# The last expert's first piece: two half loads cut by partitions, the second laid out in eight blocks of eight rows

## The chip, the core and the metric

The kernel runs on one core of one Trainium2 chip. The metric is device time in microseconds; three runs of the kernel before gave 1342.24, 1344.37 and 1346.36, a median of 1344.37. TensorE is PE in the rows, VectorE DVE, ScalarE ACT, GpSimd POOL, and SP is the engine whose queue issues the loads.

## The reference

One layer of a streaming encoder trunk on 256 tokens and 16 meta tokens of width 1024: a mixer (gated DeltaNet beside gated linear attention) and then a mixture of 64 experts, of which every token takes two. Of the mixture:

```python
def expert_block(args):
    xblk, e = args
    hid = jax.nn.silu(xblk @ w1[e]) * (xblk @ w3[e])
    return hid @ w2[e]
...
y = jnp.zeros((T, d), yb.dtype).at[stok].add(yb[slot] * sw[:, None].astype(yb.dtype))
...
return rmsnorm(h, norm_final)[:, N_META:]
```

Each expert has w1 and w3 of 1024 x 512 and w2 of 512 x 1024, all float32: 6 MB an expert, 403 MB for all 64.

## The kernel before

The mixer takes the first 400 us or so. Then comes a loop over the 64 experts (`for e in range(NE)`), which runs all of them, whatever the router chose, each on a small block of gathered tokens. The weights come through the tensor `wx`, which `layout` builds on the host as 64 experts x 3 pieces x 128 partitions x 4096 columns. Piece 0 holds the first half of the depth of w1 (columns 0 to 2047) and of w3 (2048 to 4095), piece 1 the second half of both, piece 2 holds w2. A piece is 2 MB: 16 KB on each of 128 partitions.

The pieces go in turn into a ring of ten buffers of 128 x 4096 (lateA to lateE, ring0 to ring4; the rows of the profile leave the number of a ring buffer out). `ring_load` issues one load or half of one from SP, `ring_more` issues as many as have a free buffer, and `ring_take` hands a piece over and gives its buffer back. Up to the last expert but one a piece is one DMA of 2 MB. The last expert's three pieces go in two halves of 1 MB each (`hf` is 0 or 1), cut by columns: for pieces 0 and 1 the halves are w1's and w3's 2048 columns, for piece 2 they are 512 output columns in each of its four blocks. Every DMA signals on one of eight semaphores in turn, and SP waits before an issue until the DMA eight places earlier has landed, and until the buffer has been read. So eight loads are in flight at most.

PE's work on the last expert, in the order in which it stands in the program: `up` on the first half of the depth (32 matmuls `h<-ring`, which read piece 0, both halves of it), 50 matmuls on zeros (`keep_warm`, `misc<-zero`), `up` on the second half of the depth (32 matmuls, which read piece 1), the gate (ACT, then DVE), one transposition, and then w2 in two halves (`y<-lateE` and `misc<-lateE` for the first 512 output columns, then `y<-lateE` and `h<-lateE` for the others), each followed by the sum into `acc`. After that come the final norm, which needs `norm_final` (loaded to `h`, issued last of the loads), and four stores.

The branch of `ring_load` that piece 0 of the last expert takes is the last one:

```python
        else:
            hs = slice(2048 * hf, 2048 * (hf + count))
            to, src = t[:, hs], src[:, hs]
```

Of the kernel before, what the change touches and what calls it, by code (L numbers as in the profile page):

```python
# [26 lines left out]
NE = 64  # L27
# [69 lines left out]
def _body(tc, a, dbg, stop, ctx, nc, V, S, G, PE):  # L97
# [62 lines left out]
    wx = a["wx"]  # L160
    nload, slab_dma, gathered, gather_after, lead, x_act, x_dve = [0], [None], [None], [None], [None], [None], [None]

    def after(cell):

        return tc.issue_after(cell[0].ins) if cell[0] is not None else ExitStack()
# [6 lines left out]
    def ring_load(n, count):  # L172

        e, part, hf = n // 6, n // 2 % 3, n % 2
        if e == SPARE // 6:
            part = (0, 2, 1)[part]
        if n == SPARE:
            ring[e, part] = [w2p.tile([P, 2048], F32, name="ys", bufs=1)]
        elif hf == 0 or n == SPARE + 1:
            slot = ring_free.pop(0)  # L180
            ring.setdefault((e, part), []).extend((slot[0].tile([P, 4096], F32, name=slot[1], bufs=1), slot))
        t = ring[e, part][-2 if n != SPARE else 0]
        src = wx[e, part]
        if n == SPARE:
            to, src = t, src[:, 0:2048]
        elif part == 2 and e == NE - 1:
            hs = slice(512 * hf, 512 * hf + 512)
            to, src = t.rearrange("p (j d) -> p j d", j=4)[:, :, hs], src.rearrange("p (j d) -> p j d", j=4)[:, :, hs]
        else:
            hs = slice(2048 * hf, 2048 * (hf + count))  # L190
            to, src = t[:, hs], src[:, hs]
        with after(slab_dma):
            nc.sync.dma_start(to, src)

    def ring_more(n=6 * NE, whole=True):
        while n and nload[0] < 6 * NE and (ring_free or (nload[0] % 2 == 1) != (nload[0] == SPARE + 1) or nload[0] == SPARE):
            i = nload[0]
            count = 2 if whole and i % 2 == 0 and i != SPARE and i < 6 * (NE - 1) else 1
            ring_load(i, count)
            nload[0] += count  # L200
            n -= 1
# [13 lines left out]
    def partC(n):  # L215
        used[0] += n
        assert used[0] <= 4096
        return lateC[:, used[0] - n:used[0]]
# [3 lines left out]
    small = acts.tile([P, 3 + 96 + 8 + 8], F32, name="small")  # L222
# [133 lines left out]
    rows = acts.tile([P, 16], F32, name="rows")  # L356
# [4 lines left out]
    src = [(h[:, 0], P, NM), (h[:, 1], P, NM + P), (xm, NM, 0)]  # L361
# [3 lines left out]
    for i in (2, 0, 1):  # L365
        x, n, col = src[i]
# [544 lines left out]
    half = acts.tile([P, 3], F32, name="half")  # L911
# [3 lines left out]
    for i in range(2):  # L915
        t = partC(256).rearrange("p (c x) -> p c x", c=2)
# [178 lines left out]
    for s in range(4):  # L1095
        p = [pip.tile([P, T], F32, name="ip") for _ in range(2)]
        for kh in range(2):
            wh, wl = parts(len(units) + 2 * s + kh, 4)
            slab_load(s0 + 2 * s + kh + SLABS - 2)
            src = slab_tile[s0 + 2 * s + kh]  # L1100
# [341 lines left out]
    for e in range(NE):  # L1442
        g, i = divmod(e, GR)
# [110 lines left out]
def blocks(w, k, n):  # L1554

    r, c = w.shape
    return w.reshape(r // (k * P), k, P, c // n, n).transpose(3, 0, 2, 1, 4).reshape(-1, P, k * n)


def layout(i):  # L1560

    small = np.concatenate([
        i["norm_head_dn"][0].reshape(1, P).T, i["norm_head_gla"][0].reshape(2, P).T,
        i["conv_dn"][0].reshape(4, 24, P).transpose(2, 1, 0).reshape(P, 96),
        i["norm_ffn"][0].reshape(KT, P).T,
        i["norm_mix"][0].reshape(KT, P).T], 1)
    rows = np.concatenate([np.broadcast_to(i[n], (P, i[n].shape[1])) for n in ("dt_bias", "a_log", "b_group", "b_router")], 1)
    w = i["w_in"][0]
    few = np.zeros((D, P), np.float32)
    few[:, 0:8], few[:, 32:40], few[:, 64:80] = w[:, O_A:O_A + 8], w[:, O_B:O_B + 8], w[:, O_LR:O_LR + 16]  # L1570
    w13 = [i[n][0].reshape(NE, 2, 4, P, 512).transpose(0, 3, 1, 2, 4).reshape(NE, P, 2, 2048) for n in ("w1", "w3")]
    wx = np.empty((NE, 3, P, 4096), np.float32)
    for part in range(2):
        for n in range(2):
            wx[:, part, :, 2048 * n:2048 * n + 2048] = w13[n][:, :, part]
    wx[:, 2] = i["w2"][0].reshape(NE, 4, P, D).transpose(0, 2, 1, 3).reshape(NE, P, 4096)
    out = {
        "x": i["x"], "meta_tokens": i["meta_tokens"], "norm_final": i["norm_final"], "small": small, "rows": rows,
        "w_in": blocks(np.concatenate([w[:, :O_A], w[:, I_GQ:O_LR], w[:, I_G1:]], 1), KT, P),
        "w_small": blocks(few, KT, P)[0],  # L1580
        "w_proj_dn": blocks(i["w_proj_dn"][0], KT, P), "w_proj_gla": blocks(i["w_proj_gla"][0], KT, P),
        "w_out": blocks(i["w_out"][0], 4, 256),
        "w_route": blocks(np.concatenate([i["w_group"][0], i["w_router"][0]], 1), KT, 72)[0],
        "w_alpha": np.concatenate([i["w_alpha"][0], i["b_alpha"]], 0), "wx": wx, "consts": CONSTS}
    return {k: np.ascontiguousarray(v) for k, v in out.items()}
# [17 lines left out]
```

## Time and profile before

| What | us |
|---|---|
| median of three runs (1342.24 to 1346.36) | 1344.37 |
| the profiled execution's own time | 1344.17 |
| its span in the trace | 1342.4 |
| PE busy | 1179.6 |
| DVE busy | 447.5 |
| ACT busy | 314.6 |
| POOL busy | 92.4 |

The time is the span and 1.8 us around it. PE is busy for 88% of the span, but its matmuls are pipelined and wait for weights in between; what set the end is read from the chain of waits, and for a change to the last loads from the last 80 us of it. A DMA's landing is the start of its issue on SP plus its time to landing.

### The profile page before, as it was taken

How to read it: one execution, taken by the hardware profiler on the slowest of the kernel's cores; microseconds unless marked ns; L12 is line 12 of the kernel's file. 1: busy time of each engine (PE TensorE's matmuls, PEld its weight loads, DVE VectorE, ACT ScalarE, POOL GpSimd, SP SyncE). 2: the span in 40 equal slices, each digit the busy share in tenths (PEclk: the TensorE clock that was granted, in tenths of full speed). 3: DMA queues.
4: the chain of work that ended last, by engine and by line, in shares of the span. 5: the costliest groups of instructions: out<-in, count | busy, mean ns of one | idle time of the engine just before them, and what ended most of it. 6: DMA issues, size and time to landing. Idle time of an engine off the chain costs nothing.

```text
span 1342.4 us, 24165 instructions
## 1 busy us (share of the span) xinstructions
PE 1179.6 (88%) x10513; PEld 760.3 (57%) x10513; DVE 447.5 (33%) x1007; ACT 314.6 (23%) x681; POOL 92.4 (7%) x163
## 2 busy tenths in 40 slices
PE   9999999999999998898878888788788878878776
PEld 8998999899997454344333434334343434334323
DVE  6689787656665222111110101111110111111101
ACT  5575565365441111101000000100000001010101
POOL 1016214502000000000000000000000000000000
PEclk8999999999999999999998898989998998999999
DMA  7633332333997999899999999999999999999995
GB/s 267 217 111 110 113 117 90 126 110 117 369 372 306 427 428 426 366 427 427 427 426 428 428 427 426 426 429 427 425 428 429 427 425 428 428 428 425 428 425 226
DMA packets 46287, 459.53 MB, mean 342 GB/s; under 512 B 5441, under 2 KB 5697, under 8 KB 20450
## 3 DMA queue, kind: packets, MB, share of 16 engines
q1 hardware_dynamic: 45890, 457.43, 83.4%
q8 instruction: 83, 1.36, 0.4%
q10 hardware_dynamic: 288, 0.52, 0.1%
q14 instruction: 26, 0.21, 0.0%
HBM read 456.89 MB, written 1.05 MB: 341 GB/s over the span
## 4 chain that ended last, share of the span: by engine, by line
DMA 44%; PE 15%; ACT 1%; DVE 1%; issue 0%; DVEq 0%; POOL 0%; SPq 0%
DMA ring<-wx 15%; DMA lateB<-wx 9%; DMA lateA<-wx 9%; DMA lateE<-wx 6%; PE acc L125 5%; PE h L125 4%; DMA lateC<-wx 3%; DMA lateD<-wx 3%; PE y L125 3%; PE misc L125 2%; ACT ys L116 1%; ACT sl L116 0%; DVE hid L1329 0%; PE misc L1334 0%; DVE hT L1336 0%
## 5 line engine op out<-in xcount | busy, mean ns | idle before, releaser
L125 PE MATMUL acc<-ys,wot 128*128 128x512 f32 x480 | 226.8, 615 | 27.6 <-ACT ys L116 26.9
L125 PEld LDWEIGHTS acc<-ys,wot 128*128 128x128 f32 x480 | 88.6, 195 | 155.6 <-issue 92.3
L1329 DVE SCALAR_TENSOR_TENSOR hid<-h,sc,sl 128x128 f32<-128x128 f32 x63 | 22.1, 350 | 451.6 <-ACT sl L116 451.6
L125 PE MATMUL ip<-xh,lateD 128*128 128x256 f32 (+2 forms) x784 | 162.3, 297 | 0.0
L116 ACT ACTIVATE sl<-h,sc 128x128 f32<-128x128 f32 x63 | 23.2, 368 | 481.5 <-PE h L125 476.1
L125 PE MATMUL h<-ring,xg 128*32 128x256 f32 x2048 | 124.9, 382 | 6.5 <-DMA ring<-wx 6.3
L125 PEld LDWEIGHTS ip<-xh,lateD 128*128 128x128 f32 x784 | 128.8, 194 | 1.9 <-issue 0.3
L125 PE MATMUL ip<-xl,lateD 128*128 128x256 f32 (+2 forms) x392 | 115.6, 295 | 0.0
L116 ACT ACTIVATE ys<-y,sc 128x512 f32<-128x512 f32 (+1 forms) x61 | 41.5, 680 | 280.4 <-PE y L125 280.4
L125 PEld LDWEIGHTS h<-ring,xg 128*32 128x32 f32 x2048 | 62.5, 110 | 74.7 <-issue 25.6
L108 DVE TENSOR_SCALAR ys<-y,sc 128x512 f32<-128x512 f32 x59 | 44.3, 750 | 167.7 <-PE y L125 167.7
L113 DVE TENSOR_TENSOR lateD<-slab,lateD 128x1024 fp32r<-128x1024 f32 x64 | 80.9, 1264 | 30.7 <-ACT lateD L116 29.4
L116 ACT ACTIVATE lateD<-slab 128x1024 fp32r<-128x1024 f32 x64 | 67.7, 1058 | 57.0 <-PE ip L125 54.7
L125 PE MATMUL y<-ring,hT 128*32 128x512 f32 x496 | 68.2, 667 | 14.4 <-DMA ring<-wx 14.0
L125 PEld LDWEIGHTS ip<-xl,lateD 128*128 128x128 f32 x392 | 75.8, 194 | 1.1 <-issue 0.3
L125 PEld LDWEIGHTS misc<-ohs,h 128*128 128x128 f32 x488 | 56.8, 191 | 22.2 <-issue 12.1
L125 PE MATMUL misc<-ohs,h 128*128 128x128 f32 x488 | 62.7, 281 | 6.4 <-DVE hT L1336 6.4
L156 POOL TENSOR_TENSOR rss<-rss,c 128x1 f32<-128x1 f32 x2 | 1.1, 556 | 925.2 <-DVE rss L103 925.2
L1334 PE MATMUL misc<-c,hid 128*128 128x128 f32 x64 | 20.8, 324 | 49.0 <-DVE hid L1329 49.0
L125 PE MATMUL ip<-xl,wh 128*128 128x256 f32 (+2 forms) x192 | 57.3, 298 | 0.0
L125 PE MATMUL ip<-xh,wh 128*128 128x256 f32 (+2 forms) x192 | 56.8, 296 | 0.0
L125 PE MATMUL ip<-xh,wl 128*128 128x256 f32 (+2 forms) x192 | 56.1, 292 | 0.0
(480 smaller groups left out, 1643.0 us busy)
## 6 DMA issues: line engine op xcount, KB each, us to landing
ring<-wx SPq DMA_DIRECT2D x90, 2048.0 KB, 39.2
lateA<-wx SPq DMA_DIRECT2D x19, 2048.0 KB, 39.2
lateD<-wx SPq DMA_DIRECT2D x19, 2048.0 KB, 39.2
slab<-w_in SPq DMA_DIRECT2D x72, 512.0 KB, 3.7
lateC<-wx SPq DMA_DIRECT2D x18, 2048.0 KB, 39.2
lateB<-wx SPq DMA_DIRECT2D x18, 2048.0 KB, 39.2
lateE<-wx SPq DMA_DIRECT2D x17, 2048.0 KB, 39.1
ring<-wx SPq DMA_DIRECT2D x12, 1024.0 KB, 8.9
```

Of the source, the lines that this page charges most:

```text
L108: e.tensor_scalar(out, in0, s1, None, op0=op0, **kw)
L113: return (eng or V).tensor_tensor(out, in0, in1, op)
L116: return S.activation(out, in_, func, **kw)
L125: return PE.matmul(out, lhsT, rhs, start=start, stop=stop, **kw)
L156: G.tensor_tensor(out, x, C(name, n)[:, :w], ALU.pow)
L1329: late_dve[0] = V.scalar_tensor_tensor(hid, ph[:, P:256], sc[:, 0:1], sl, op0=ALU.mult, op1=ALU.mult)
L1334: PE.transpose(p[:, 0:P], hid, ident)
```

## The change

Only the two loads of piece 0 of the last expert (`e == NE - 1`, `part == 0`) change. Before, each moved 128 partitions of 2048 columns, 8 KB a partition, from `wx`. Now they are cut by partitions: the first moves partitions 0 to 63 with all their 4096 columns (64 rows of 16 KB) from `wx`, the second partitions 64 to 127 from a new input `w_half`. That one has the shape 8 x 9 x 4096, of which 8 x 8 rows are filled and read: the ninth row of each block keeps the eight blocks from being one run of 64 rows. Both loads still move 1 MB into the same buffer, and PE reads it as before. `w_half` is the first of the kernel's inputs; `wx` keeps its own copy of the rows.

```diff
         elif part == 2 and e == NE - 1:
             hs = slice(512 * hf, 512 * hf + 512)
             to, src = t.rearrange("p (j d) -> p j d", j=4)[:, :, hs], src.rearrange("p (j d) -> p j d", j=4)[:, :, hs]
+        elif part == 0 and e == NE - 1:
+            to, src = t[64 * hf:64 * hf + 64], (src[0:64], a["w_half"][:, 0:8])[hf]
         else:
...
+    half = np.zeros((8, 9, 4096), np.float32)
+    half[:, 0:8] = wx[NE - 1, 0, 64:].reshape(8, 8, 4096)
     out = {
-        "x": i["x"], "meta_tokens": i["meta_tokens"], "norm_final": i["norm_final"], "small": small, "rows": rows,
+        "w_half": half, "x": i["x"], "meta_tokens": i["meta_tokens"], "norm_final": i["norm_final"], "small": small, "rows": rows,
```

On SP the end of the program, from the last piece of expert 62 on, stood like this before (a row ends with the shape that is written):

```order
L193 DMA lateD<-wx 128x4096
L193 DMA ring_10397<-wx 128x2048 x2
L193 DMA ring_10457<-wx 128x2048 x2
L193 DMA lateE<-wx 128x4x512 x2
L1482 DMA h<-norm_final 128x1024
```

And in the changed program, on the same engine from the same place:

```order
L195 DMA lateD<-wx 128x4096
L195 DMA ring_10397<-wx 64x4096
L195 DMA ring_10397<-w_half 64x1x4096
L195 DMA ring_10457<-wx 128x2048 x2
L195 DMA lateE<-wx 128x4x512 x2
L1484 DMA h<-norm_final 128x1024
```

Two rows have taken the place of one pair; nothing has moved past another instruction, here or on another engine.

## Rows read from the trace of the kernel before

**Rows 1.** The page: the chain of work that ended last, as shares of the span, by engine and by line.

```profile
DMA 44%; PE 15%; ACT 1%; DVE 1%; issue 0%; DVEq 0%; POOL 0%; SPq 0%
DMA ring<-wx 15%; DMA lateB<-wx 9%; DMA lateA<-wx 9%; DMA lateE<-wx 6%; PE acc L125 5%; PE h L125 4%; DMA lateC<-wx 3%; DMA lateD<-wx 3%; PE y L125 3%; PE misc L125 2%; ACT ys L116 1%; ACT sl L116 0%; DVE hid L1329 0%; PE misc L1334 0%; DVE hT L1336 0%
```

**Rows 2.** The same chain in order of time, its last 125 us: start and length in us, and what it was.

```profile
1219.21 39.30 DMA lateA<-wx
...
1258.59 40.24 DMA lateB<-wx
1298.84 0.14 issue
1298.97 2.02 PE y L125 x16
...
1301.78 7.13 PE acc L125 x16
1308.91 3.63 PE h L125 x64
...
1316.92 3.70 PE acc L125 x8
1320.62 1.86 PE h L125 x32
1322.48 2.90 PE misc L125 x50
1325.38 1.91 PE h L125 x32
...
1336.20 0.75 DVE xg L103
```

**Rows 3.** Stretches of 2 to 100 us: start and end, length, busy us of PE, PEld, DVE, ACT and POOL with their instructions, PE's granted clock, the mean busy share of the 16 DMA engines, GB/s.

```profile
900.00:1000.00 100.00, 79.74 (x702) 37.78 (x694) 15.50 (x33) 8.47 (x16) 0.00 (x0) 0.98 1.01 427
1100.00:1200.00 100.00, 84.48 (x701) 41.40 (x702) 16.06 (x35) 9.77 (x18) 0.00 (x0) 0.93 1.01 427
...
1318.00:1320.00 2.00, 2.00 (x6) 0.83 (x5) 0.00 (x0) 0.00 (x0) 0.00 (x0) 1.00 1.01 398
1320.00:1322.00 2.00, 2.00 (x30) 0.94 (x32) 0.00 (x0) 0.00 (x0) 0.00 (x0) 1.00 0.77 311
1322.00:1324.00 2.00, 2.00 (x41) 1.59 (x30) 0.00 (x0) 0.00 (x0) 0.00 (x0) 1.00 0.57 211
1324.00:1326.00 2.00, 2.00 (x40) 1.64 (x41) 0.00 (x0) 0.00 (x0) 0.00 (x0) 1.00 0.52 201
1326.00:1328.00 2.00, 1.25 (x24) 0.51 (x16) 0.28 (x1) 0.37 (x1) 0.00 (x0) 1.00 0.52 204
1328.00:1330.00 2.00, 1.40 (x17) 0.56 (x17) 0.38 (x3) 0.40 (x1) 0.00 (x0) 1.00 0.15 59
```

**Rows 4.** The timeline of SP, the last seven loads: start of the issue and its length in us. In this order: piece 0 of the last expert (two loads to a ring buffer), piece 1 (two), piece 2 (two to lateE), norm_final.

```profile
1278.13 0.33 SPq L193 DMA_DIRECT2D ring<-wx  x1
1284.19 0.33 SPq L193 DMA_DIRECT2D ring<-wx  x1
1289.12 0.33 SPq L193 DMA_DIRECT2D ring<-wx  x1
1293.96 0.33 SPq L193 DMA_DIRECT2D ring<-wx  x1
1298.90 0.66 SPq L193 DMA_DIRECT2D lateE<-wx  x1
1303.74 5.47 SPq L193 DMA_DIRECT2D lateE<-wx  x1
1309.32 1.84 SPq L1482 DMA_DIRECT2D h<-norm_final  x1
```

**Rows 5.** DMA issues in narrow stretches, one for each of those loads in the same order, and how many us it took from issue to landing; for the fourth of them (issued at 1293.96) the trace gives no landing.

```profile
ring<-wx SPq DMA_DIRECT2D x1, 1024.0 KB, 37.9
ring<-wx SPq DMA_DIRECT2D x1, 1024.0 KB, 34.3
ring<-wx SPq DMA_DIRECT2D x1, 1024.0 KB, 31.9
...
lateE<-wx SPq DMA_DIRECT2D x1, 1024.0 KB, 27.3
lateE<-wx SPq DMA_DIRECT2D x1, 1024.0 KB, 25.1
h<-norm_final SPq DMA_DIRECT2D x1, 512.0 KB, 20.7
```

**Rows 6.** The timeline of PE on the last expert: start and length in us, and in brackets the idle time before and who ended it.

```profile
1320.55 1.93 PE L125 MATMUL h<-ring,xg 128*32 128x256 f32 x32
1322.42 2.97 PE L125 MATMUL misc<-zero 128*128 128x128 bf16 x50
1325.31 1.93 PE L125 MATMUL h<-ring,xg 128*32 128x256 f32 x32
...
1328.83 0.64 PE L125 MATMUL y<-lateE,hT 128*32 128x256 f32 x8 [0.38 <-DVE hT L1336]
...
1331.63 0.64 PE L125 MATMUL y<-lateE,hT 128*32 128x256 f32 x8
```

**Rows 7.** The only load that writes a part of the partitions from many rows, 16 of 128: lateA from meta_tokens, issued at 0.71 us. Its row of the DMA issues (us to landing last), and the stretch in which it ran, with the columns of rows 3.

```profile
lateA<-meta_tokens SPq DMA_DIRECT2D x1, 64.0 KB, 2.1
...
1.70:2.20 0.50, 0.50 (x7) 0.50 (x6) 0.00 (x0) 0.49 (x2) 0.49 (x2) 1.00 0.47 131
```

## The prediction

> **What bounds the kernel now.** I read the chain of waits first. By engine, DMA has 44% of the span and PE 15%, and the lines of DMA are the loads of `wx` [rows 1]: over the experts the kernel waits for weights. The stretches say how: from 900 to 1000 us and from 1100 to 1200 us all 16 DMA engines are busy (share 1.01) and move 427 GB/s [rows 3]. There a megabyte costs 1,048,576 / 427,000 = 2.46 us, a 2 MB piece 4.91.
>
> But the change touches only the last expert's first piece, and what counts is whether the chain still goes through DMA there. It does not. In order of time the last DMA of the chain is the load of lateB, issued at 1258.59, 40.24 us long, over at 1298.84; from 1298.97 on the chain is PE, ACT and DVE to the end [rows 2]. [...] What follows is 43.6 us of compute to the end of the span at 1342.4, and it moves only if a load that was early becomes late.
>
> How early are they? Issue plus time to landing [rows 4, 5]: piece 0 lands at 1278.13 + 37.9 = 1316.0 and 1284.19 + 34.3 = 1318.5; piece 1 at 1289.12 + 31.9 = 1321.0 for its first half; piece 2 at 1298.90 + 27.3 = 1326.2 and 1303.74 + 25.1 = 1328.8; norm_final at 1309.32 + 20.7 = 1330.0. The second half of piece 1 has no landing in the trace; I put it halfway between its neighbours, at 1323.6. PE uses piece 0 from 1320.55, piece 1 from 1325.31, piece 2 from 1328.83 and 1331.63 [rows 6], and DVE norm_final at 1336.20 [rows 2]. The slacks are therefore 2.05 us, 1.7, 2.6, 2.8 and 6.2. PE shows no wait for a DMA at any of these places; ahead of piece 1 it runs its 50 matmuls on zeros from 1322.42 [rows 6].
>
> One more view matters: how the DMA engines finish. Their share is 1.01 up to 1320, falls to 0.77 and 0.57 up to 1324, stays at 0.52 for the two stretches to 1328 and is 0.15 in the last [rows 3]. A share of a half for 4 us says that about eight of the 16 engines were done with all loads by 1324 or earlier and the other eight still had to work to 1329: a leading and a lagging half, some 7 us apart. A load has landed when the slowest engine has done its part, so the landings above are those of the lagging half. The rows don't name the engines of either half.
>
> **The change, part by part.**
>
> *The first load*, 64 rows of 16 KB for 128 of 8 KB: the same megabyte. On 16 engines it is four rows of 16 KB each, the row length of the 2 MB pieces that stream at 427 GB/s [rows 3]. Cost 0.
>
> *The second load* on eight engines: 128 KB on each of these, nothing on the others. At 2.46 us for 64 KB an engine this is +2.46 us of work for the eight that get it and -2.46 us for the other eight, and all loads behind it in the queue (piece 1, piece 2, norm_final) shift with it on each engine. Two ends follow. If the eight are the leading half, they have 7 us to spare and the lagging half is relieved: landings from this load on come up to 2.46 us earlier. PE was not waiting, so the end gains 0. If the eight are, or contain some of, the lagging half, the landings come 2.46 us later: piece 0 at 1318.5 + 2.46 = 1320.96 against the use at 1320.55, +0.41; piece 1 at 1323.6 + 2.46 = 1326.06 against 1325.31, +0.75 in total and not on top of the first; piece 2 at 1328.66 and 1331.26 against 1328.83 + 0.75 and 1331.63 + 0.75, nothing more; norm_final at 1332.5 against 1336.2, nothing. So this term lies between 0 and +0.8 us. I take 0: the slack covers nearly all of either case. What hides the later landing is PE's own work, above all the 2.9 us of matmuls on zeros ahead of piece 1; without that cover the loaded lagging half would cost the whole 2.46.
>
> [...]
>
> *Issue on SP.* Two issues replace two. A plain load holds SP for 0.33 us, the loads of another form 0.66 and 5.47 [rows 4]; I take 0.33 to 0.66, with 5.47 as the bound. Even that ends at 1284.19 + 5.47 = 1289.66, and the next issue stood at 1289.12: it would slip by 0.5 us, with its data first wanted some 30 us later [rows 5]. Nothing behind it on SP but loads with that same lead. Below nothing the term cannot go: SP is on no part of the chain [rows 1]. Cost 0.
>
> *Order and waits.* No instruction changes place on any engine and no wait is added. The buffer is the same, and PE still waits for both loads. A store later waits for the semaphore that the second load signals, at 1338, long after. Cost 0.
>
> *A new input ahead of the others* moves where `wx` lies in memory. The two 100 us stretches read different parts of `wx` at the same 427 GB/s [rows 3], so I see no dependence on the place; bounds of 0.5% either way of the 870 us of expert stream, 4 us, go into the rivals.
>
> Sum against the profiled execution: 1344.17 + 0 (0 to 0.8). That execution lies 0.20 below the median, so against the median 1344.4, at most 1345.2.
>
> **The rivals.**
>
> 1. *Slower: the two cut loads share the way into the buffer.* Each writes only half of the partitions, and on the first all 16 engines write into 64 of them. If two engines that write to the same group of partitions take turns, a packet takes twice its time. For the lagging half the first load then takes 4.92 instead of 2.46 us (+2.46), and if the eight engines of the second load lag too, their 128 KB take up to 9.8 us instead of 2.46 (+7.4), since the others write their own loads to the same partitions meanwhile. Together +9.8: piece 0 would land at 1328.3, 7.8 us after its use at 1320.55, and the end would come 7.8 us later, at 1352.2. The rival decides from the point where the landing slips by more than the slack of 2.05 us, and beats 0.3% (4 us) from a slip of 6. Against it: the load of 16 rows to 16 partitions landed in 2.1 us and moved 131 GB/s over its half microsecond [rows 7], where an eighth of the partitions, taking turns, would give 427 / 8 = 53. For it: that load is tiny, 64 KB, and the megabytes behind one another here are not. It also needs the lagging engines among the eight; if the eight lead, the waiting falls on engines with 7 us to spare and the relieved ones are late by little more than their slack.
>
> [...]
>
> 2. *Faster: PE waits for these loads in most executions, only not in this one.* Then relieving the lagging half brings up to 2.46 us: 1344.4 - 2.5 = 1341.9. Against it stand slacks of 1.7 us and more at all places [rows 4 to 6]. It would stay within 0.3%.
>
> 3. *It doesn't do what it says:* the second load still runs on 16 engines. Then it is 64 KB an engine as before, and the time 1344.4.
>
> 4. *The place of `wx` in memory* changes the stream's rate by 0.5%: 1340 or 1348.
>
> **How the numbers follow.** Forecast (landings move, the end by 0 to 0.8 us): 0.72. Rival 1: 0.13. Rival 2: 0.07. Rival 3: 0.03. Rival 4: 0.05, half on each side. About 0.3% is what a measurement of this kernel can tell from no change; that is 4 us. Within it lie the forecast and rivals 2 and 3: 0.82. Slower by more: rival 1 and half of rival 4, 0.155, written 0.15. Faster by more: half of rival 4, 0.025, written 0.03. The predicted time is the forecast's 1344.4. The range takes in rival 2 at 1341.9, the forecast's 1345.2 and the scatter of the three runs around their median (about 2 us up): 1341.7 to 1347.4. Outside it are rival 1 and rival 4, 0.18.
>
> **What the profile after would show.** The chain's last DMA should again be the load of expert 61's last piece, over at about 1299, and PE's matmuls of the last expert should show no wait for a DMA, or one of under 1 us ahead of the first 32. The end of the loads tells the halves: if the leading half got the megabyte, the time in which the DMA share is near a half shrinks by some 5 us (one side +2.46, the other -2.46) and norm_final lands near 1327.6; if the lagging half got it, that stretch grows and norm_final lands near 1332.5. Rival 1 shows as a wait of several us for the ring buffer ahead of PE's first 32 matmuls and as GB/s well under 400 while other loads are still queued. Rival 2 would show the last expert's waits gone in a time that fell by 2 us. Rival 4 would show in the GB/s of 900 to 1200 us. I would be wrong if PE waits over 4 us for piece 0, or if the stream up to 1299 is not what it was.

## The result and the profile after

| What | before | after |
|---|---|---|
| median of six runs, us | 1341.57 (1338.76 to 1346.36) | 1357.79 (1352.58 to 1364.45) |
| ratio, with its 95% interval | | 1.0131 (1.0099 to 1.0163) |
| the profiled execution's own time, us | 1344.17 | 1359.62 |
| its span, us | 1342.4 | 1357.7 |

The change costs 16.2 us by the medians and 15.45 us between the two profiled executions. That is slower by four times what a measurement can tell from no change, and outside the predicted range. The ratio is estimated apart from the medians, here and in the experiments, and need not be their quotient. The first rival came true, at twice its price.

**Where the rate went.** Stretches of the kernel after, with the columns of [rows 3]:

```profile
900.00:1000.00 100.00, 80.31 (x724) 39.30 (x722) 15.31 (x34) 7.78 (x15) 0.00 (x0) 0.98 1.01 427
1100.00:1200.00 100.00, 85.22 (x702) 41.02 (x700) 15.41 (x33) 9.41 (x17) 0.00 (x0) 0.93 1.01 428
...
1296.00:1300.00 4.00, 3.14 (x14) 1.25 (x7) 0.75 (x1) 0.69 (x1) 0.00 (x0) 1.00 1.08 418
1300.00:1304.00 4.00, 4.00 (x11) 1.71 (x9) 0.00 (x0) 0.00 (x0) 0.00 (x0) 1.00 1.01 217
1304.00:1308.00 4.00, 2.37 (x34) 0.94 (x32) 0.00 (x0) 0.00 (x0) 0.00 (x0) 1.00 0.98 211
1308.00:1312.00 4.00, 2.37 (x32) 0.97 (x32) 0.24 (x1) 0.37 (x1) 0.00 (x0) 0.79 1.00 207
1312.00:1316.00 4.00, 0.48 (x1) 0.18 (x1) 0.41 (x2) 0.00 (x0) 0.00 (x0) 0.50 1.10 216
1316.00:1320.00 4.00, 0.00 (x0) 0.00 (x0) 0.00 (x0) 0.00 (x0) 0.00 (x0) 0.50 0.93 148
1320.00:1324.00 4.00, 3.66 (x16) 0.75 (x16) 0.00 (x0) 0.00 (x0) 0.00 (x0) 0.51 0.97 208
...
1332.00:1336.00 4.00, 1.56 (x16) 0.90 (x20) 0.00 (x0) 0.00 (x0) 0.00 (x0) 0.50 0.81 247
1336.00:1340.00 4.00, 4.00 (x59) 2.83 (x52) 0.00 (x0) 0.00 (x0) 0.00 (x0) 0.80 0.56 214
```

The expert stream is what it was: 427 and 428 GB/s. At 1300 us it breaks in two: the share of the DMA engines stays near 1.0, but they deliver 217 GB/s, 0.51 of 427. Engines that are busy all the time and move half as much have packets that take twice their time. The packets in the trace, which no view lists one by one, say so themselves: of the 86 packets of 16 KB that start from 1301 to 1308 us none took less than 1.02 us and the middle one 1.24, where the middle one of the kernel before, from 1280 to 1304 us, took 0.61. This is the reverse of what [rows 3] show at the end of the kernel before, where the GB/s fall with the share because half of the engines have nothing left to do. Reading the two last columns together tells the two apart.

**Which loads it took.** SP's timeline of the kernel after (start of the issue, its length), which answers to [rows 4]; lateB stands first to place this execution beside the other:

```profile
1254.24 0.33 SPq L195 DMA_DIRECT2D lateB<-wx  x1
...
1264.11 0.33 SPq L195 DMA_DIRECT2D lateA<-wx  x1
1268.91 0.33 SPq L195 DMA_DIRECT2D lateD<-wx  x1
1273.79 0.58 SPq L195 DMA_DIRECT2D ring<-wx  x1
1279.75 0.73 SPq L195 DMA_DIRECT2D ring<-w_half  x1
...
1310.07 25.14 SPq L1484 DMA_DIRECT2D h<-norm_final  x1
```

And the DMA issues of the kernel after in narrow stretches (KB each, us from issue to landing), which answer to [rows 5]. For the load of `w_half` the trace gives no landing here.

```profile
lateA<-wx SPq DMA_DIRECT2D x1, 2048.0 KB, 44.8
...
lateD<-wx SPq DMA_DIRECT2D x1, 2048.0 KB, 51.3
...
ring<-wx SPq DMA_DIRECT2D x1, 1024.0 KB, 51.0
...
h<-norm_final SPq DMA_DIRECT2D x1, 512.0 KB, 35.4
```

lateA and lateD are whole loads, issued ahead of the changed ones, and nothing about them was changed. A whole load took 40.24 us in the kernel before [rows 2]; these took 44.8 and 51.3. The first cut load took 51.0 where it had taken 37.9 [rows 5], and norm_final landed at 1310.07 + 35.4 = 1345.5 where it had landed at 1330.0: 15.5 us later, about what lies between the two executions.

**How it reached the end.** The chain of waits of the kernel after in order of time (start, length, what), which answers to [rows 2]:

```profile
1264.11 44.79 DMA lateA<-wx
...
1308.94 2.40 PE h L125 x32
...
1312.65 7.55 another core or an unknown queue
...
1320.34 3.74 PE y L125 x16
...
1328.56 5.75 another core or an unknown queue
...
1334.44 3.47 PE h L125 x32
```

The two pieces of "unknown queue" are told by PE's timeline of the kernel after (in brackets the idle time and who ended it), which answers to [rows 6]:

```profile
1308.94 2.37 PE L125 MATMUL h<-lateA,xg 128*32 128x256 f32 x32 [2.58 <-DMA lateA<-wx]
...
1320.34 3.67 PE L125 MATMUL y<-lateD,hT 128*32 128x512 f32 x16 [7.69 <-DMA lateD<-wx]
...
1334.44 3.47 PE L125 MATMUL h<-ring,xg 128*32 128x256 f32 x32 [5.88 <-DMA ring<-w_half]
1337.84 2.96 PE L125 MATMUL misc<-zero 128*128 128x128 bf16 x50
1340.74 1.93 PE L125 MATMUL h<-ring,xg 128*32 128x256 f32 x32
```

PE waits 2.6 and 7.7 us for two loads that the change does not touch and 5.9 us for the one on eight engines. From 1334.44 on everything follows as before. The first 32 matmuls on piece 0 started at 1320.55 in the kernel before [rows 6] and start 13.9 us later now; they take 3.47 us and not 1.93, at a granted clock of 0.50 (the stretch from 1332 to 1336 us, and before it those from 1312 to 1324) where it had been 1.00 [rows 3]. 13.9 + 1.5 = 15.4 us, the whole difference between the two executions.

It is not the whole price. The kernel after issued lateB at 1254.24 and the kernel before at 1258.59 [rows 2], so this execution was 4.35 us ahead when the change began to tell. Such a lead is scatter between executions: in the experiments that differ in the last expert's loads alone, lateB was issued anywhere from 1249.98 (run 10) to 1261.03 us (run 8). Counted from lateB's issue to the end of the span the change costs (1357.7 - 1254.24) - (1342.4 - 1258.59) = 19.7 us: 16.2 us of waits (2.6 + 7.7 + 5.9) and, within 0.2 us, 3.7 us at the lower clock (0.4, 1.7 and 1.5 us on the three groups of matmuls that follow them). The interval of the ratio, 13 to 22 us, holds 15.4 and 19.7 alike.

### The profile page after: what moved, and what is told of

Read it like the earlier page. It is cut to its first block, busy times and chain, and to the rows that moved or that the text cites. A ratio compares the mean times of both kernels' runs of the same rounds, so it can differ in the third digit from the quotient of the medians.

```text
span 1357.7 us, 24165 instructions
## 1 busy us (share of the span) xinstructions
PE 1180.0 (87%) x10513; PEld 758.9 (56%) x10513; DVE 447.0 (33%) x1007; ACT 314.1 (23%) x681; POOL 91.7 (7%) x163
## 2 busy tenths in 40 slices
DMA packets 46151, 459.53 MB, mean 338 GB/s; under 512 B 5433, under 2 KB 5689, under 8 KB 20442
## 4 chain that ended last, share of the span: by engine, by line
DMA 47%; PE 12%; another core or an unknown queue 1%; DVE 1%; ACT 1%; issue 0%; DVEq 0%; POOL 0%; SPq 0%
DMA ring<-wx 20%; DMA lateA<-wx 12%; DMA lateE<-wx 9%; DMA lateB<-wx 6%; PE h L125 4%; PE acc L125 4%; PE y L125 2%; PE misc L125 2%; ACT ys L116 0%; ACT sl L116 0%; DVE hid L1331 0%; PE misc L1336 0%; DVE hT L1338 0%; PE misc L1310 0%
## 5 line engine op out<-in xcount | busy, mean ns | idle before, releaser
L125 PE MATMUL y<-ring,hT 128*32 128x512 f32 x496 | 67.5, 660 | 13.9 <-DMA ring<-wx 13.4
```

Source lines behind the costliest of these rows:

```text
L125: return PE.matmul(out, lhsT, rhs, start=start, stop=stop, **kw)
```

## The experiments

All edit the same branch of `ring_load`. The first four were to tell the prediction's first rival (the cut loads share the way into the buffer) from a theory that blames the eight engines alone. The texts of the first four call them theories 1 and 2, the later ones A and B. The kernel before ran at 1342.32, 1340.04 and 1340.10 us on the chips of the three sets (runs 1 to 4, 5 to 8, 9 to 11).

**1. Cut at partition 64, all on 16 engines.** Both halves from `wx`.

```diff
+        elif part == 0 and e == NE - 1:
+            to, src = t[64 * hf:64 * hf + 64], src[64 * hf:64 * hf + 64]
```

> Both loads of the last expert's first piece cut by partitions (0 to 63, 64 to 127) as in the changed kernel, but the second also as 64 rows from wx on sixteen engines. Theory 1 (a load that writes only one half of the partitions halves the rate of everything in flight): as slow as the changed kernel or nearly, 8 to 20 us over the kernel before, with a stretch of 205 to 220 GB/s at a DMA share near 1.0 after 1300 us and a wait of PE for piece 0. Theory 2 (the confinement to eight engines is what costs): within 2 us of the kernel before, no stretch at half the rate. Theory 3 (the reads of four neighbouring rows by an engine are what costs): as theory 1.

Measured: 1351.44 us, ratio 1.0092 (1.0058 to 1.0126). Stretches of this kernel:

```profile
1296.00:1300.00 4.00, 3.98 (x10) 1.84 (x11) 0.01 (x1) 0.00 (x0) 0.00 (x0) 1.00 1.07 303
1300.00:1304.00 4.00, 4.00 (x28) 1.71 (x30) 0.00 (x0) 0.00 (x0) 0.00 (x0) 1.00 1.01 221
...
1320.00:1324.00 4.00, 3.15 (x11) 1.36 (x8) 0.75 (x1) 0.69 (x1) 0.00 (x0) 0.93 0.98 202
```

The half rate is there without any load on eight engines (5441 packets under 512 B, as in the kernel before). Eight engines are not needed for it.

**2. Eight engines, all partitions.** The first load as before; the second moves w3's columns of all 128 partitions from a copy in eight blocks, 128 KB on each of eight engines.

```diff
+        elif part == 0 and e == NE - 1 and hf:
+            to, src = t[:, 2048:], a["w_half"][:, 0:16]
...
+    half = np.zeros((8, 17, 2048), np.float32)
+    half[:, 0:16] = wx[NE - 1, 0, :, 2048:].reshape(8, 16, 2048)
```

> The first load as in the kernel before; the second (w3's 2048 columns of all 128 partitions) from a copy of 8 blocks of 16 rows, so that it runs on eight engines but writes all partitions. Theory 1 (half of the partitions): 0 to 1 us over the kernel before, the DMA rate above 390 GB/s until the leading engines are done. Theory 2 (eight engines): 10 us or more over, with a stretch at half the rate. Theory 3 (neighbouring rows on the read side): 0 to 1 us.

Measured: 1349.52 us, ratio 1.0057 (1.0032 to 1.0083). A stretch of this kernel:

```profile
1304.00:1308.00 4.00, 2.80 (x49) 1.23 (x41) 0.35 (x1) 0.37 (x1) 0.00 (x0) 1.00 1.00 227
```

The half rate is there again. Theory 1 expected no loss here and was wrong: a load that writes all partitions can have it too.

**3. Every second partition.** Two loads of 64 rows again, but the even partitions and then the odd ones.

```diff
+        elif part == 0 and e == NE - 1:
+            to, src = t.rearrange("(p n) c -> n p c", n=2)[hf], src.rearrange("(p n) c -> n p c", n=2)[hf]
```

> Piece 0 of the last expert in two loads of 64 rows again, but the first writes the even partitions and the second the odd ones, both on sixteen engines. Theory 1 (which half of the partitions is written decides): no loss, 0 to 1 us, since every second partition reaches both halves. A form of it in which the mere number of 64 partitions decides: 8 to 20 us. Theory 2 (eight engines): 0.

Measured: 1340.30 us, ratio 0.9989 (0.9963 to 1.0014). Stretches of this kernel:

```profile
1300.00:1304.00 4.00, 2.83 (x18) 0.98 (x19) 0.99 (x2) 0.69 (x1) 0.00 (x0) 1.00 1.01 426
1304.00:1308.00 4.00, 4.00 (x11) 1.76 (x10) 0.00 (x0) 0.00 (x0) 0.00 (x0) 1.00 1.02 430
1308.00:1312.00 4.00, 4.00 (x42) 1.84 (x44) 0.00 (x0) 0.00 (x0) 0.00 (x0) 1.00 0.98 416
```

Nothing is lost. Not the number of rows, nor two loads of half the partitions, but which partitions they are decides.

**4. The cut at 64, at expert 32.** The same pair as in run 1, in the middle of the stream (the last expert as before).

```diff
+        elif part == 0 and e == 32:
+            for n in range(2):
+                with after(slab_dma):
+                    nc.sync.dma_start(t[64 * n:64 * n + 64], src[64 * n:64 * n + 64])
+            return
```

> The last expert as in the kernel before; instead the first piece of expert 32 goes in two loads of 64 rows, partitions 0 to 63 and 64 to 127, on sixteen engines each. Theory 1: a stretch at half the rate in the middle of the stream that lasts as long as in the changed kernel, some 25 to 35 us, and since the stream is the bound there, half of that lost for good: 10 to 18 us over the kernel before. Theory 2: 0 to 1 us. If the loss belongs to the end of the program alone (few loads left to fill in), 0 to 3 us.

Measured: 1349.54 us, ratio 1.0044 (1.0025 to 1.0063), about 5.9 us. Stretches of this kernel:

```profile
844.00:848.00 4.00, 4.00 (x24) 1.67 (x26) 0.00 (x0) 0.00 (x0) 0.00 (x0) 1.00 1.00 424
848.00:852.00 4.00, 2.83 (x56) 1.34 (x47) 0.00 (x0) 0.00 (x0) 0.00 (x0) 1.00 1.08 360
...
856.00:860.00 4.00, 0.00 (x0) 0.00 (x0) 0.00 (x0) 0.00 (x0) 0.00 (x0) 0.50 1.04 209
...
868.00:872.00 4.00, 4.00 (x33) 1.66 (x36) 0.00 (x0) 0.00 (x0) 0.00 (x0) 0.88 0.99 414
```

It is no matter of the end of the kernel. Two loads of 1 MB hold the whole stream at half its rate for some 16 us, then it is back; theory 1 expected some 25 to 35 us and a loss of 10 to 18. The stretch is shorter than in run 1 (some 27 us), and so, it seems, is the loss; the two intervals overlap a little.

**5. Reading or writing.** Written to every second partition, as in run 3, but read from a copy in which each load's 64 rows lie behind one another, as in run 1.

```diff
+        elif part == 0 and e == NE - 1:
+            to, src = t.rearrange("(p n) c -> n p c", n=2)[hf], a["w_half"][64 * hf:64 * hf + 64]
...
+    half = wx[NE - 1, 0].reshape(64, 2, 4096).transpose(1, 0, 2).reshape(P, 4096).copy()
```

> The read side taken apart from the write side. The two loads write every second partition, as in the run with rows two apart, which lost nothing (0.9989), but they read from a copy of the piece in which the 64 rows of each load lie behind one another, as the two loads cut at partition 64 read theirs. If it is the reading that slows (64 neighbouring rows in memory), the loss of the cut at 64 comes back: about +9 to +12 us, half the rate from 1300 us on, 1351 to 1354 against 1342. If it is the writing (which engine writes to which partitions), no loss: within 0.3% of the kernel before, 410 GB/s and more up to 1318 us.

Measured: 1341.09 us, ratio 0.9999 (0.9970 to 1.0028), with 406, 430 and 396 GB/s in the three stretches of 4 us from 1300 to 1312 us. So for loads on 16 engines it is the writing. For those on eight engines no run takes reading and writing apart. A copy as the first of the inputs costs nothing either.

**6. One block further.** Partitions 8 to 127 in one load, 120 rows of 16 KB, so that its blocks of eight rows lie one block further than those of a whole load; then partitions 0 to 7, 128 KB.

```diff
+        elif part == 0 and e == NE - 1:
+            to, src = (t[8:128], t[0:8])[hf], (src[8:128], src[0:8])[hf]
```

> [...] Theory A: a load is slow when it writes only a half of the partitions. Then this one is all but whole and loses nothing: within 0.4% of the kernel before. Theory B: eight engines alone do it. No loss either, since the second load is an eighth of a megabyte (under 1 us). Theory C: each engine has a block of eight partitions of its own in the whole loads (engine 0 has 0 to 7, engine 1 has 8 to 15), and a load in which engines write to the blocks of others makes all packets in flight take twice their time, since some engines are ahead of the others. Then this load costs as much as the cut at 64 or more: +6 to +15 us, 1348 to 1357, and a rate of 200 to 300 GB/s in the 15 us from about 1300 us on.

Measured: 1352.12 us, ratio 1.0095 (1.0067 to 1.0122). The rate in this kernel:

```profile
1304.00:1308.00 4.00, 3.54 (x36) 1.32 (x34) 0.00 (x0) 0.00 (x0) 0.00 (x0) 1.00 1.01 223
1308.00:1312.00 4.00, 1.93 (x32) 0.94 (x32) 0.24 (x1) 0.37 (x1) 0.00 (x0) 1.00 0.94 211
```

120 of 128 partitions, and as dear as a cut in half. Theory A, as a matter of half of the partitions, falls. Theory B fell in run 1; it expected no loss here and is wrong again. How many engines the 120 rows go on, and which engine takes which rows, no view shows.

**7 and 8. Eight engines, on blocks 0 to 7 or on blocks 8 to 15.** The first load as before; the second moves w3's columns of 64 partitions alone, on eight engines, and TensorE sums piece 0 of the last expert over these 64 rows. Run 7 has partitions 0 to 63, run 8 has 64 to 127. Half of piece 0 stays out of the sum: w1's other 64 rows are loaded and not used, w3's are not loaded. By theory C run 7 writes the eight engines' own blocks and run 8 those of the other eight; that the eight engines are those of blocks 0 to 7 is the author's assumption.

```diff
+        elif part == 0 and e == NE - 1 and hf:
+            to, src = t[0:64, 2048:], a["w_half"][:, 0:8]
...
+            r = slice(0, 64) if nload[0] == 6 * NE and (NE - 1, 1) not in ring and k < 4 else slice(0, P)
...
-                lead[0] = mm(ph[32 * j:32 * j + 32, 0:256], xg[:, k, cols], w[:, :, k % 4, j * P:j * P + P],
+                lead[0] = mm(ph[32 * j:32 * j + 32, 0:256], xg[r, k, cols], w[r, :, k % 4, j * P:j * P + P],
```

> [...] The first load (w1's columns, 128 partitions, 16 engines) is that of the kernel before. [...] Theory B (eight engines alone) and theory A (half of the partitions) have half the rate for some 5 to 10 us and +3 to +8 us. Theory C (blocks of others) has no loss: within 0.3% of the kernel before, 400 GB/s and more up to 1315 us.

> [...] It leaves out w3's rows on partitions 0 to 63, and TensorE sums the first piece of the last expert over partitions 64 to 127. Theories A and B expect the same time of both runs. Theory C has a loss here alone: half the rate while these 64 KB an engine are under way, from about 1301 us for 5 to 10 us, and +3 to +8 us against the other run.

Measured: 1352.35 us, ratio 1.0072 (1.0047 to 1.0097), and 1353.40 us, ratio 1.0095 (1.0069 to 1.0120). One stretch of each, run 7 and then run 8:

```profile
1304.00:1308.00 4.00, 2.23 (x37) 1.04 (x29) 0.64 (x2) 0.37 (x1) 0.00 (x0) 1.00 0.97 248
```

```profile
1312.00:1316.00 4.00, 3.04 (x56) 1.33 (x44) 0.12 (x1) 0.37 (x1) 0.00 (x0) 1.00 0.96 217
```

Theory C expected 400 GB/s and more of run 7 and was wrong, with 248 GB/s at a share of 0.97: blocks of eight neighbouring partitions are not what an engine has for its own, provided that the assumption holds, which no view shows. The conclusion rests on the rates and not on the two times: in both runs PE also has another order, with the 8 matmuls to `acc` behind those on piece 0 and not ahead of them, so that they no longer cover the wait for `w_half` (3.4 and 4.0 us).

**9 and 10. Which rows.** The pair has the same number of loads and bytes and differs in the distance of the rows. The odd rows go in one load; the even rows go in four loads of 256 KB on 16 engines, in run 9 as 16 rows eight apart, in run 10 as 32 rows four apart with half of the columns.

```diff
+        elif part == 0 and e == NE - 1:
+            def rows(x, n, i):
+                return x.rearrange("(p n) c -> n p c", n=n)[i]
+            for to, src in [(rows(t, 8, 2 * n), rows(src, 8, 2 * n)) for n in range(4)] if hf else [(rows(t, 2, 1), rows(src, 2, 1))]:
```

> Theory C (a block of eight neighbouring partitions for each engine) fell with the eight engines in their own blocks, which lost as much as those in other blocks. [...] Here the odd rows go first, in one load of 64 rows (harmless in two runs), then the even rows in four loads of 16 rows that lie eight apart, one row on each of the 16 engines. By blocks of eight neighbours every engine is at home here, and nothing is lost: within 0.3% of the kernel before. [...]

> The other of the pair: the odd rows in one load of 64 rows first, then the even rows again in four loads of 256 KB each, but each of 32 rows that lie four apart (half of the columns), two rows on each engine. The number of loads, their bytes and the bytes of each engine are those of the run with rows eight apart. [...] If small loads, more loads or rows that are not neighbours are what costs, it loses as much as the run with rows eight apart.

Measured: run 9 1344.43 us, ratio 1.0031 (1.0007 to 1.0055); run 10 1341.61 us, ratio 1.0012 (0.9991 to 1.0032). Stretches of run 9:

```profile
1300.00:1304.00 4.00, 4.00 (x11) 1.65 (x9) 0.00 (x0) 0.00 (x0) 0.00 (x0) 1.00 1.08 348
1304.00:1308.00 4.00, 3.98 (x65) 1.98 (x64) 0.00 (x0) 0.00 (x0) 0.00 (x0) 1.00 0.95 231
```

and of run 10:

```profile
1300.00:1304.00 4.00, 4.00 (x65) 1.99 (x64) 0.00 (x0) 0.00 (x0) 0.00 (x0) 1.00 1.00 422
1304.00:1308.00 4.00, 2.28 (x17) 0.63 (x17) 0.99 (x3) 0.70 (x2) 0.00 (x0) 1.00 0.87 341
```

PE's timeline at the same matmuls, run 9 and then run 10:

```profile
1312.97 3.67 PE L125 MATMUL y<-lateD,hT 128*32 128x512 f32 x16 [3.79 <-DMA lateD<-wx]
```

```profile
1305.59 1.95 PE L125 MATMUL y<-lateD,hT 128*32 128x512 f32 x16 [0.38 <-DVE hT L1343]
```

Run 9 has 231 GB/s at a share of 0.95, and PE waits 3.8 us for lateD. Run 10's dip is of the other kind: 341 GB/s at a share of 0.87 is 392 for a full one, so engines had nothing to do for a moment, and PE does not wait for lateD. The intervals of the two ratios overlap; it is the rates and the wait that tell the runs apart. As many loads, bytes and engines, and only the rows eight apart lose the rate. Blocks of eight neighbours, by which run 9 would lose nothing, fall again; and small loads, more loads or rows that are not neighbours are not what costs, since run 10 has all of them.

**11. The change's megabyte on eight engines, cut by even and odd.**

```diff
+        elif part == 0 and e == NE - 1:
+            to, src = t.rearrange("(p n) c -> n p c", n=2)[hf], (src.rearrange("(p n) c -> n p c", n=2)[0], a["w_half"][:, 0:8])[hf]
...
+    half = np.zeros((8, 9, 4096), np.float32)
+    half[:, 0:8] = wx[NE - 1, 0, 1::2].reshape(8, 8, 4096)
```

> What the change does (a megabyte on eight engines, laid out as eight blocks of eight rows with a gap), but with the two loads cut by even and odd partitions and not at partition 64. The first load (even rows, 16 engines) is harmless. If eight engines can be kept apart by this (each at partitions that no other writes at the time), only the 128 KB an engine remain, and the time is that of the kernel before within 0.3%, as my prediction had it for the change. [...]

Measured: 1353.37 us, ratio 1.0088 (1.0066 to 1.0111). PE's timeline of this kernel:

```profile
1313.60 1.95 PE L125 MATMUL y<-lateD,hT 128*32 128x512 f32 x16 [2.34 <-DMA lateD<-wx]
...
1324.68 3.64 PE L125 MATMUL h<-ring,xg 128*32 128x256 f32 x32 [4.57 <-DMA ring<-w_half]
```

The same odd rows that cost nothing on 16 engines in run 3 halve the rate on eight (244, 227 and 225 GB/s in the three stretches of 4 us from 1300 to 1312 us, at shares of 1.06, 1.01 and 1.00), and PE waits for the same two loads as in the kernel after. So the change has two parts that each do it: the cut at partition 64 (run 1, 0.92%) and the layout for eight engines (runs 2 and 11, 0.57% and 0.88%). By the ratios it is open whether the two add up: their sum, 1.5 to 1.8%, lies about at the upper end of the change's own interval (0.99 to 1.63%).

The lead of one execution over another drops out if the profiled executions are counted from lateB's issue, as above. Against the kernel before they then lost 11.7 us (run 1), 12.5 (2), 1.3 (3), -0.2 (5), 10.9 (6), 4.8 (9), -0.2 (10) and 12.6 (11), one execution each. So counted, runs 9 and 10 lie apart, and the two parts of the change (11.7 and 12.5) cost more apart than the change does (19.7).

None of these is faster than the kernel before. The harmless ones (3, 5, 10) are within 0.3% of it, as one would expect where the stream of whole loads sets the time.

## Why the prediction was wrong

**What bounds the kernel** was read rightly: the stream is at 427 and 428 GB/s in both kernels, and all that was lost was lost behind 1299 us.

**The step that failed** is "*The first load*, ... four rows of 16 KB each, the row length of the 2 MB pieces that stream at 427 GB/s. Cost 0", and with it the 2.46 us for 64 KB an engine on which the second load's term was built. No row of the trace before shows that this load runs on eight engines; the packet counts below do. Row length does not make a load alike: run 1, in which both loads are cut at 64 and nothing else is changed, cost 12.3 us. What the runs show in its place is that such a load doubles the time of every packet in flight, those of whole loads included (217 GB/s at a share of 1.01, and 1.24 us for the middle packet of 16 KB where it had been 0.61). No view shows the reason. The ±2.46 us that the eight engines were to gain or lose is no more than a part of it.

**The first rival** named the cause, which partitions the loads write, and half of the price. That loads ahead of the cut ones slow down with them was not in it. Its two terms were good: the lagging half was to take 2.46 us more for the first load and 7.4 for the second. Measured, as us from issue to landing against the kernel before [rows 2, 5]: lateA 44.8 - 40.24 = +4.6, lateD 51.3 - 40.24 = +11.1, first cut load 51.0 - 37.9 = +13.1, second 1334.31 - 1279.75 - 34.3 = +20.3 (its landing is the end of the chain's second unknown piece, 1328.56 + 5.75). So the first cut load added 2.0 and the second 7.2. What was missing are the 11.1 us ahead of them. That all loads behind the second one shift with it on each engine was the author's estimate: no run shows in what order an engine takes its packets, only that these loads landed in the order of their issue (1308.9, 1320.2, 1324.8, 1334.3 and norm_final at 1345.5). Up to 1298.84 nothing changed. But the rate fell at 1300 us, and lateA landed only at 1264.11 + 44.8 = 1308.9: by the prediction's own estimate of two halves some 7 us apart, the leading engines could be in the first cut load while the lagging ones still had lateA and lateD to write. No view names the engines. 20.3 less the 4.4 us by which this execution issued the load earlier (1279.75 against 1284.19) and less the slack of 2.05 leave the 13.9 us, to rounding, by which the matmuls on piece 0 start later; 1.5 us of slow clock come on top.

**The evidence against that rival was misread.** The small load of 16 rows moved 131 GB/s [rows 7], and the text set 427 / 8 = 53 against it, as if every partition counted alike. The runs show that they do not: 64 rows moved 426 GB/s in run 3, two apart, and 221 in run 1, as neighbours. With 64 KB at a share of 0.47 the row proves little either way, and it was no evidence against the rival. The prediction gave it 0.13, which was too little for a rival against which no other row spoke.

**The terms of no cost** held or did not matter. The two cut loads hold SP for 0.58 and 0.73 us (0.33 to 0.66 was taken). The bound of 5.47 us did not hold for the issues behind them, up to 10.6 us for a load of lateE and 25.14 for norm_final, behind which nothing waits but the stores. The stream's rate, and with it rival 4, did not move (427 and 428 GB/s; run 5 with a copy as the first input, ratio 0.9999). Rival 2 (faster) did not come, and neither did rival 3 (still on 16 engines). The packets of the whole trace, the kernel before and then the kernel after:

```profile
DMA packets 46287, 459.53 MB, mean 342 GB/s; under 512 B 5441, under 2 KB 5697, under 8 KB 20450
```

```profile
DMA packets 46151, 459.53 MB, mean 338 GB/s; under 512 B 5433, under 2 KB 5689, under 8 KB 20442
```

There are eight packets under 512 B fewer. Run 1, with all loads on 16 engines, has 5441 again, run 4 with one load more 5457, and runs 9 and 10 with three more 5489: these counts fit one such packet for each engine that takes part in a load, 16 for each load more, so the second load ran on eight (and those of runs 2, 7 and 8 too, with 5433). The second load's 7.2 us, those of 128 KB an engine at twice the price, agree.

**Which rows cost.** On 16 engines, 64 neighbouring rows lose (221 GB/s in run 1, 209 in run 4), and rows eight apart (231 in run 9); rows two apart do not (426 to 430 in run 3, 396 to 430 in run 5), nor rows four apart (422 in run 10). 120 neighbouring rows from partition 8 on lose too (223 in run 6). On eight engines every layout tried loses: 227 GB/s with all partitions (run 2), 248 and 217 with 64 neighbouring ones (runs 7 and 8), 227 with the odd ones (run 11). No view here shows how the rows are dealt out to the engines, so what sets the two kinds of rows apart was not shown.

**What stays open.** Why does everything in flight slow down, whole loads as well? If only the leading eight engines' packets took twice their time, the rate would be three quarters of 427, 320 GB/s; it is 217 from the first stretch on, none of the 86 packets of 16 KB from 1301 to 1308 us keeps its old 0.61 us, and lateA, a whole load, lands 4.6 us late. Why a load to some of the rows slows all engines was not tried. That engines get in each other's way at the partitions, the first rival's idea, agrees with the dependence on the rows that are written, but no view shows two engines at the same partitions.

## What to carry to other kernels

Cut a load by columns, or take rows two or four apart (426 and 422 GB/s here); a cut at partition 64, a load shifted by eight partitions or one spread over eight engines halved the rate of everything in flight (221, 223 and 227 GB/s), here for 16 to 36 us for 2 MB of such loads. A change to a late load can slow loads that were issued before it (here by 4.6 and 11.1 us), so a stretch's slack must be held against the whole queue in flight and not against the changed load alone. Where GB/s fall at a DMA share of 1.0, as here at 217 GB/s, look at which partitions each load writes; where both fall together, as at the end of the kernel before, look at who had nothing to do.

## What the runs showed of the hardware that was not expected

- A few loads with the wrong rows halve the rate of all 16 DMA engines, whole loads in flight included: 427 to 217 GB/s at the end, 424 to 209 in the middle of the stream, where it is back (414) some 16 us later.
- With 2 MB cut at 64 in both cases the half rate lasted some 16 us at expert 32 and some 27 us at the end, where the kernel lost 5.9 and 12.3 us (0.44% and 0.92%), 0.37 and 0.46 of the stretch. What sets its length no view shows.
- 64 partitions can be written at the full rate: 416 to 430 GB/s for rows two apart (run 3), 221 for neighbouring rows (run 1).
- TensorE's granted clock was 0.50 after a wait of 7.7 us, and the 16 matmuls behind it took 3.67 us; in run 11, after a wait of 2.3 us at a clock of 1.00, the same 16 took 1.95.
